# Three weight-chunk splits and the gate-weight splits reordered around the first norm's row factor

## The chip, the cores and the metric

The kernel runs on one core of one Trainium2 chip. Its time is the device time of one execution in microseconds (us), and of several executions the median counts. The engines of the core run side by side, each in the order of its own instruction list, and wait for one another by semaphores: PE is the matrix engine (TensorE), DVE is VectorE, ACT is ScalarE, POOL is GpSimd, and SP issues most of the DMAs.

## The reference

One layer of an encoder on a sequence of 512 tokens of width 1024, all in float32. What matters here is its first part:

```
h    = rms_norm(x, attn_norm_g)
proj = h @ w_in                                  # 1024 -> 2560
xr, gate, q, k, v = split(proj)                  # 512 columns each
xr   = centred_depthwise_conv(xr, conv_w, conv_b)   # 4 taps
h_f  = rg_lru(xr, wa_fwd, ba_fwd, wx_fwd, ...)   # two sigmoid gates, then a scan
h_b  = rg_lru(xr, wa_bwd, ba_bwd, wx_bwd, ...)   # the same, backwards
```

After it come attention, the output projection and the MLP (`relu(h @ w_up)^2 @ w_down`) and a final norm; the change does not touch their code.

## The kernel before

Every float32 product is made of three matmuls. An operand is split into a rounded high part and the remainder (the "rest", or low part), and the helper `mm3` (L222) adds high x high, high x low and low x high in one accumulator. A weight arrives in chunks of 128 x 1024. `emit_dma` (L182) loads a chunk into one of three `wraw` buffers; `conv_hi(i)` (L189) makes the high part `whi` of chunk i on ACT; `conv_lo(i)` (L195) makes its rest `wlo` on DVE and then issues the load of the next chunk into the buffer that it has freed. `whi` and `wlo` have four buffers each.

The list of chunks begins with three that come together with x (0 to 2), then chunk 3 (the last quarter of the columns of xr) and chunks 4 to 7 (the columns of v). Chunks 3, 4 and 5 are loaded first; chunk 6 is loaded when chunk 3 has been split, chunk 7 after chunk 4, chunk 8 after chunk 5.

The order of PE, ACT, DVE and POOL is that of the program text. The stretch around the change goes as follows.

- The first norm is applied late: the products use x times the gain, and the row factor 1/sqrt(mean square + eps) multiplies the results. `rstd_cols` (L305) makes the factor per token as `rcol`: a small DVE instruction `rv`, then a power on POOL (L310). `row_tile` (L313) transposes it on PE (`prow`, L302) and ACT copies it to SBUF as `rrow` (L316). This row is `rstd`.
- `conv_a(t)` (L374) multiplies the t-th quarter of xr, which lies in a PSUM bank, by `rstd` on DVE (`xr`, L376), and ACT makes the first tap `xc` of it (L378). `conv_b(t)` (L381) adds the three other taps with three DVE instructions (L383 to L385). `conv_h(t)` (L387) makes the high part `xch` on ACT, `conv_c(t)` (L391) its rest `xcl` on DVE.
- `gate_weights(t)` (L365) splits the recurrence's gate weights of quarter t: the high part `gwh` on ACT (L368), the rest `gwl` on POOL (L369).
- `next(spc)` (L553) emits thirteen small POOL instructions (`pl`, `sp`, `cneg`, `chalf`, L139 to L145) for two constants of the recurrence.
- `xmm(ks)` (L544) are steps of the fourth quarter of xr on PE.
- Then comes the v loop of 32 steps (L593), each an `mm3`; chunk 4 serves steps 0 to 7, chunk 5 steps 8 to 15. At steps 5, 6, 8, 9, 11, 12, 14 and 15 two gate products `pg` each are woven in (`lru_gate`, L395): sixteen in all, four for each quarter. ACT turns each `pg` into a sigmoid `ga` (L401).

Four PSUM banks (tag "pj") serve the four quarters `pxr` first and then the gate products in turn. So gate product n needs bank n mod 4: the first four wait for the `xr` instructions of quarters 0 to 3, every later one for the sigmoid four products before it. The sigmoids stand in ACT's list in this order: the table load for the sigmoid, two `ga` of quarter 0, `xch` of quarter 2, two more `ga` of quarter 0, `xch` of quarter 3, `conv_hi(6)`, four `ga` of quarter 1, and so on.

Of the kernel before, what the change touches and what calls it, by code (L numbers as in the profile page):

```python
# [72 lines left out]
def hybrid_kernel(ctx: ExitStack, tc, xw, xT, w_in, w_v, w_out, w_up, w_dn, gates, vecs, rel, onehot, fg, out):  # L73
# [13 lines left out]
    def g_(name, dt=FT, shape=(P, S)):  # L87
        return work.tile(list(shape), dt, name=name, tag="g", bufs=NG)
# [4 lines left out]
    def ps_(name, tag):  # L93
        return psum.tile([P, S], FT, name=name, tag=tag, bufs={"pj": 4, "gs": 2, "et": 2}[tag])

    def f(t):
        return t.bitcast(FT)
# [22 lines left out]
    def softplus_consts():  # L120
        ts, tt = nc.gpsimd.tensor_scalar, nc.gpsimd.tensor_tensor
        lam = vt[:, VEC["lam"]:VEC["lam"] + 8]
        e8, sp, z, z2, pl = [small(n, 8) for n in ("e8", "sp8", "z8", "z28", "pl8")]
        cneg = consts.tile([P, 8], FT, name="cneg")
        chalf = consts.tile([P, 8], FT, name="chalf")
        stt(e8, lam, -1.0, lam, op0=OP.mult, op1=OP.max)
        nc.vector.tensor_scalar(sp, lam, -1.0, 0.0, op0=OP.mult, op1=OP.max)
        yield
        act(e8, e8, AF.Exp, scale=-1.0)
        yield  # L130
        nc.vector.tensor_scalar(z, e8, 2.0, None, op0=OP.add)
        nc.vector.reciprocal(z, z)
        tt(z, z, e8, op=OP.mult)
        tt(z2, z, z, op=OP.mult)
        ts(pl, z2, 1.0 / 19, 1.0 / 17, op0=OP.mult, op1=OP.add)
        for c in (15, 13, 11, 9, 7, 5, 3, 1):
            if c == 7:
                yield
            tt(pl, pl, z2, op=OP.mult)  # L139
            ts(pl, pl, 1.0 / c, None, op0=OP.add)  # L140
        tt(pl, pl, z, op=OP.mult)
        ts(pl, pl, 2.0, None, op0=OP.mult)
        tt(sp, pl, sp, op=OP.add)
        ts(cneg, sp, -LRU_C, None, op0=OP.mult)
        ts(chalf, sp, 0.5 * LRU_C, None, op0=OP.mult)  # L145
        yield cneg, chalf

    spc = softplus_consts()
# [28 lines left out]
    def wblock(h, b, q):  # L177
        return w_dn[h, int(b[1]) - 1, (int(b[0]) - 1) * NQ + q]
# [3 lines left out]
    def emit_dma():  # L182
        if plain:
            i = plain.popleft()
            r = stream.tile([P, 1024], FT, name="wraw", tag="wraw", bufs=3)
            nc.sync.dma_start(r, wblock(*chunks[i]) if isinstance(chunks[i], tuple) else chunks[i])
            raws[i] = r

    def conv_hi(i):  # L189
        if i < len(chunks):  # L190
            hi = stream.tile([P, 1024], FR, name="whi", tag="whi", bufs=4)
            act(hi, raws[i], AF.Copy)  # L192
            splits[i] = (hi,)

    def conv_lo(i):  # L195
        if i < len(chunks):
            r = raws.pop(i)
            lo = stream.tile([P, 1024], FR, name="wlo", tag="wlo", bufs=4)
            nc.vector.tensor_tensor(lo, r, f(splits[i][0]), op=OP.subtract)  # L199
            splits[i] += (lo,)  # L200
            c = chunks[i]
            if isinstance(c, tuple) and c[1][0] == "s":
                nxt = {"s1": ("s2", "22"), "s2": ("s4", "21")}.get(c[1])
                if nxt:
                    nc.gpsimd.dma_start(r, wblock(c[0], nxt[1], c[2]), accum_op=OP.add)  # L205
                    raws[C_UP + c[0] * CH + HF + {"s2": 2 * NQ + 2 * c[2], "s4": 6 * NQ + c[2]}[nxt[0]]] = r
            else:
                emit_dma()

    def feed(c, k):  # L210
        if k == 2:
            conv_hi(c + 3)
        elif k == 4:
            conv_lo(c + 3)
# [7 lines left out]
    def mm3(o, a, b, first, last):  # L222
        nc.tensor.matmul(o, lhsT=a[0], rhs=b[0], start=bool(first), stop=False)  # L223
        nc.tensor.matmul(o, lhsT=a[0], rhs=b[1], start=False, stop=False)  # L224
        nc.tensor.matmul(o, lhsT=a[1], rhs=b[0], start=False, stop=bool(last))  # L225
# [119 lines left out]
    def bias_prep():  # L345
        for i in range(2):
            pbz = ps_("pbias", "pj")
            nc.tensor.matmul(pbz[0:NH, :], lhsT=relt, rhs=oht[i], start=True, stop=True)
            nbs = g_("nbs", shape=(NH, S))
            nc.vector.tensor_scalar(nbs, pbz[0:NH, :], -1.0, None, op0=OP.mult)  # L350
            nc.scalar.dma_start(nbd[:, i * S:(i + 1) * S], nbs)
# [3 lines left out]
    def load_tw(h):  # L355
        t = work.tile([P, 1024], FT, name="tw", tag="tw", bufs=4)[:, :896]
        ap = bass.AP(tensor=nbd.tensor, offset=nbd.offset + h * 2 * S, ap=[[1, P], [1, 896]])
        nc.sync.dma_start(t, ap)
        tws[h] = t
# [5 lines left out]
    def gate_weights(t):  # L365
        raw = gwr.pop(t)
        hi, lo = g_("gwh", FR), g_("gwl", FR)
        act(hi, raw, AF.Copy)  # L368
        nc.gpsimd.tensor_tensor(lo, raw, f(hi), op=OP.subtract)  # L369
        gwt[t] = (hi, lo)  # L370
# [3 lines left out]
    def conv_a(t, pp):  # L374
        xr = g_("xr")
        nc.vector.tensor_tensor(xr, pp, rstd, op=OP.mult)  # L376
        c = g_("xc")
        act(c, xr, AF.Identity, scale=vec("w2", t), bias=vec("cb", t))  # L378
        xrt[t], xc[t] = xr, c

    def conv_b(t):  # L381
        xr, c = xrt.pop(t), xc[t]
        stt(c[:, 2:], xr[:, :S - 2], vec("w0", t), c[:, 2:], op0=OP.mult, op1=OP.add)  # L383
        stt(c[:, 1:], xr[:, :S - 1], vec("w1", t), c[:, 1:], op0=OP.mult, op1=OP.add)
        stt(c[:, :S - 1], xr[:, 1:], vec("w3", t), c[:, :S - 1], op0=OP.mult, op1=OP.add)  # L385

    def conv_h(t):  # L387
        xch[t] = g_("xch", FR)
        act(xch[t], xc[t], AF.Copy)

    def conv_c(t):  # L391
        xcl[t] = g_("xcl", FR)
        nc.vector.tensor_tensor(xcl[t], xc[t], f(xch[t]), op=OP.subtract)

    def lru_gate(t, m):  # L395
        hi, lo = gwt[t]
        pg = ps_("pg", "pj")
        sl = slice(m * P, (m + 1) * P)
        mm3(pg, (hi[:, sl], lo[:, sl]), (xch[t], xcl[t]), True, True)
        o = g_("ga")  # L400
        act(o, pg, AF.Sigmoid, bias=vec(("ba0", "bx0", "ba1", "bx1")[m], t))  # L401
        gact[t, m] = o
# [141 lines left out]
    def xmm(ks):  # L544
        for k in ks:
            mm3(pxr[3], wk(3, k), hk(k), k == 0, k == KD - 1)

    conv_hi(3)
    conv_lo(3)
    gate_weights(0)  # L550
    conv_hi(4)
    gate_weights(1)
    cneg, chalf = next(spc)  # L553
    xmm((0,))
    rstd = row_tile(rcol, "et")
    conv_a(0, pxr[0])
    conv_a(1, pxr[1])
    gate_weights(2)
    conv_lo(4)
    xmm((1, 2, 3, 4))  # L560
    conv_b(0)
    conv_h(0)
    conv_a(2, pxr[2])
    gate_weights(3)
    conv_hi(5)
    xmm((5, 6))
    conv_c(0)
    conv_b(1)
# [8 lines left out]
    def lru_hooks(n):  # L577
        m = n - GA
        if m in (11, 12, 14, 15):
            lru_x({11: 0, 12: 1, 14: 2, 15: 3}[m])  # L580
        if m in (12, 13, 20, 22):
            lru_exp({12: 0, 13: 1, 20: 2, 22: 3}[m])
        if m in (16, 17, 27, 28):
            t = {16: 0, 17: 1, 27: 2, 28: 3}[m]
            lru_sqrt(t)
            scans.extend(scan_ops(t)[:4])
        if n in SC:
            scans.popleft()()
# [4 lines left out]
    for n, (k, tt) in enumerate(steps):  # L593
        c = C_V + k // 2
        if k == 0:
            pv[tt] = ps_("pv", vtag[tt])
        hi, lo = splits[c]
        sl = slice((k % 2) * S, (k % 2 + 1) * S)
        tsl = slice(tt * P, (tt + 1) * P)
        mm3(pv[tt], (h_hi[:, k, tsl], h_lo[:, k, tsl]), (hi[:, sl], lo[:, sl]), k == 0, k == KD - 1)  # L600
        if n >= 16:
            feed(c, n % 8)
        if n in (8, 11, 14):
            conv_hi({8: 6, 11: 7, 14: 8}[n])
        if n in (9, 12, 15):
            conv_lo({9: 6, 12: 7, 15: 8}[n])
        if n >= GA and n < GA + 12 and (n - GA) % 3:
            t, m = (n - GA) // 3, 2 * ((n - GA) % 3 - 1)
            lru_gate(t, m)
            lru_gate(t, m + 1)  # L610
        if n == 0:
            conv_lo(5)
            conv_b(2)
        if n == 2:
            conv_b(3)
        if n == GA + 1:
            conv_h(2)
            conv_c(2)
        if n == GA + 2:
            conv_h(3)  # L620
            conv_c(3)
        lru_hooks(n)
        if n == 18:
            bias_prep()
            load_tw(0)
            load_tw(1)
# [665 lines left out]
```

## Time and profile before

| | |
|---|---|
| time, median of 3 runs | 569.79 us (569.21 to 570.31) |
| the profiled execution's own time | 569.28 us |
| its span in the profile | 567.5 us |
| instructions | 6886 |
| granted TensorE clock, mean | 0.996 |
| HBM read, over the span | 78.81 MB, 143 GB/s |

The profile counts microseconds from the start of the span. A row of its timeline gives start and duration in us, engine, line, operation, output and inputs with their shapes, and how many instructions of one kind are merged in the row ("x2"). A bracket at the end tells how long the engine stood idle before the instruction and what ended the wait. A row of a table of stretches gives, for each engine, its busy time in the stretch and its number of instructions.

### The profile page before, as it was taken

What the parts mean: (1) busy time and instruction counts of PE and PEld (TensorE: products, weight loads), DVE (VectorE), ACT (ScalarE), POOL (GpSimd) and SP (SyncE); (2) the same over time, 40 slices, a digit from 0 to 9 for tenths busy, and PEclk for the clock granted to TensorE, in tenths of its full rate; (3) what the DMA queues carried; (4) which work ended last, traced back from release to release, by engine and by line L of the source; (5) the groups of instructions that cost most, each with busy time, mean ns of one, the idle gap of its engine ahead of it and who ended that gap; (6) DMA issues with size and microseconds to landing.
All of it is one profiled execution on the core that took longest, in us unless ns stands there. A gap on an engine that the chain in (4) does not pass through costs nothing.

```text
span 567.5 us, 6886 instructions
## 1 busy us (share of the span) xinstructions
PE 555.4 (98%) x2520; PEld 444.8 (78%) x2520; DVE 388.8 (69%) x610; ACT 313.7 (55%) x510; POOL 50.1 (9%) x70
## 2 busy tenths in 40 slices
PE   9999999999999999999999999999999999999993
PEld 7877788677777768888888888888888888888782
DVE  6696499986865429553468778978243676896894
ACT  7659993687865525245354466653223243665654
POOL 3450000000000000000002133001000000131000
PEclk9999999999999999999999999999999999999998
DMA  7623424453261112242239799959623234699603
GB/s 261 233 74 113 147 102 142 110 160 121 75 223 38 51 59 77 76 148 75 79 111 288 173 268 273 262 174 254 196 74 112 74 112 94 196 252 262 161 1 148
DMA packets 25494, 82.97 MB, mean 146 GB/s; under 512 B 3106, under 2 KB 3234, under 8 KB 25460
## 3 DMA queue, kind: packets, MB, share of 16 engines
q1 hardware_dynamic: 19968, 64.50, 33.1%
q0 software_dynamic: 4608, 16.78, 15.5%
q10 hardware_dynamic: 884, 1.25, 0.6%
q8 instruction: 20, 0.33, 0.2%
q14 instruction: 14, 0.11, 0.1%
HBM read 78.81 MB, written 2.13 MB: 143 GB/s over the span
## 4 chain that ended last, share of the span: by engine, by line
PE 80%; DVE 10%; DMA 4%; ACT 3%; issue 2%; SPq 0%; ACTq 0%; DVEq 0%
PE pu L223 10%; PE pu L224 10%; PE pu L225 10%; PE pd L224 6%; PE pd L223 6%; PE pd L225 6%; PE pqk L223 3%; PE pwo L223 3%; DVE wlo L199 3%; PE pav L751 3%; PE pqk L225 3%; PE pwo L225 3%; PE pwo L224 3%; PE pqk L224 3%; PE pt L718 2%; DMA wraw<-in_w_dn_dram 2%
## 5 line engine op out<-in xcount | busy, mean ns | idle before, releaser
L199 DVE TENSOR_TENSOR wlo<-wraw,whi 128x1024 fp32r<-128x1024 f32 x81 | 99.9, 1234 | 38.4 <-ACT whi L192 38.3
L192 ACT ACTIVATE whi<-wraw 128x1024 fp32r<-128x1024 f32 x81 | 85.5, 1055 | 40.0 <-PE pd L225 17.7
L223 PE MATMUL pu<-h2h,whi 128*128 128x512 f32 x256 | 100.4, 392 | 0.0
L225 PE MATMUL pu<-h2h,wlo 128*128 128x512 f32 x256 | 99.7, 390 | 0.0
L224 PE MATMUL pu<-h2l,whi 128*128 128x512 f32 x256 | 99.6, 389 | 0.0
L224 PE MATMUL pd<-wlo,ah 128*128 128x512 f32 x192 | 74.8, 390 | 0.4 <-DVE wlo L199 0.4
L223 PE MATMUL pd<-whi,ah 128*128 128x512 f32 x192 | 74.7, 389 | 0.0
L225 PE MATMUL pd<-whi,al 128*128 128x512 f32 x192 | 74.7, 389 | 0.0
L1015 ACT ACTIVATE a<-pu 128x512 f32<-128x512 f32 x32 | 19.0, 598 | 97.9 <-PE pu L225 97.9
L1016 DVE TENSOR_TENSOR a<-a 128x512 f32<-128x512 f32 x32 | 22.0, 691 | 65.8 <-ACT a L1015 65.8
L225 PEld LDWEIGHTS pu<-h2h,wlo 128*128 128x128 f32 x256 | 48.0, 188 | 10.1
L223 PEld LDWEIGHTS pu<-h2h,whi 128*128 128x128 f32 x256 | 48.1, 188 | 9.8
L224 PEld LDWEIGHTS pu<-h2l,whi 128*128 128x128 f32 x256 | 48.1, 188 | 9.7
L224 PEld LDWEIGHTS pd<-wlo,ah 128*128 128x128 f32 x192 | 36.0, 188 | 8.1 <-DVE wlo L199 0.8
L223 PEld LDWEIGHTS pd<-whi,ah 128*128 128x128 f32 x192 | 36.0, 188 | 7.5
L225 PEld LDWEIGHTS pd<-whi,al 128*128 128x128 f32 x192 | 36.0, 188 | 7.5
L192 ACT ACTIVATE whi<-ts 128x1024 fp32r<-128x1024 f32 x24 | 25.5, 1060 | 23.7 <-PE pd L225 17.7
L199 DVE TENSOR_TENSOR wlo<-ts,whi 128x1024 fp32r<-128x1024 f32 x24 | 29.3, 1221 | 8.4 <-ACT whi L192 8.0
L223 PE MATMUL pqk<-h_hi,whi 128*128 128x512 f32 x64 | 26.5, 414 | 0.0
L205 POOL DMA_DIRECT2D ts<-in_w_dn_dram x16 | 16.9, 1203 | 106.7 <-DVE wlo L199 106.7
L223 PE MATMUL pwo<-yh,whi 128*128 128x512 f32 x64 | 26.3, 412 | 0.0
L720 ACT ACTIVATE ett<-pt 128x512 f32<-128x512 f32 x32 | 17.3, 591 | 15.7 <-PE pt L718 15.7
(210 smaller groups left out, 1029.5 us busy)
## 6 DMA issues: line engine op xcount, KB each, us to landing
wraw<-in_w_up_dram SPq DMA_DIRECT2D x32, 512.0 KB, 3.3
wraw<-in_w_dn_dram SPq DMA_DIRECT2D x24, 512.0 KB, 6.7
ts<-in_w_dn_dram POOLq DMA_DIRECT2D x24, 512.0 KB, 12.1
wraw<-in_w_in_dram SPq DMA_DIRECT2D x13, 512.0 KB, 3.3
wraw<-in_w_out_dram SPq DMA_DIRECT2D x8, 512.0 KB, 3.3
ts<-in_w_dn_dram SPq DMA_DIRECT2D x8, 512.0 KB, 4.9
tw<-in_w_dn_dram SPq DMA_DIRECT2D x8, 512.0 KB, 6.2
tw<-in_w_dn_dram POOLq DMA_DIRECT2D x8, 512.0 KB, 11.4
```

The lines of the kernel that those rows point to most:

```text
L192: act(hi, raws[i], AF.Copy)
L199: nc.vector.tensor_tensor(lo, r, f(splits[i][0]), op=OP.subtract)
L205: nc.gpsimd.dma_start(r, wblock(c[0], nxt[1], c[2]), accum_op=OP.add)
L223: nc.tensor.matmul(o, lhsT=a[0], rhs=b[0], start=bool(first), stop=False)
L224: nc.tensor.matmul(o, lhsT=a[0], rhs=b[1], start=False, stop=False)
L225: nc.tensor.matmul(o, lhsT=a[1], rhs=b[0], start=False, stop=bool(last))
L718: nc.tensor.transpose(pt[:, qt * P:(qt + 1) * P], en[h][qt][:, jt * P:(jt + 1) * P], ident)
L720: act(t, pt, AF.Copy)
L751: nc.tensor.matmul(pav[p][a, :], lhsT=vs[:, jt, h * DH:(h + 1) * DH], rhs=et.pop((h, jt)), start=jt == 0, stop=jt == 3)
L1015: act(r, p, AF.Relu)
L1016: nc.vector.tensor_tensor(r, r, r, op=OP.mult)
```

## The change

```diff
-    conv_hi(3)
-    conv_lo(3)
+    for i in (3, 4, 5):
+        conv_hi(i)
+    for i in (3, 4, 5):
+        conv_lo(i)
     gate_weights(0)
-    conv_hi(4)
     gate_weights(1)
-    cneg, chalf = next(spc)
     xmm((0,))
     rstd = row_tile(rcol, "et")
     conv_a(0, pxr[0])
     conv_a(1, pxr[1])
     gate_weights(2)
-    conv_lo(4)
+    gate_weights(3)
+    cneg, chalf = next(spc)
     xmm((1, 2, 3, 4))
     conv_b(0)
     conv_h(0)
     conv_a(2, pxr[2])
-    gate_weights(3)
-    conv_hi(5)
     xmm((5, 6))
...
         if n == 0:
-            conv_lo(5)
             conv_b(2)
```

No instruction is added or removed; PE's list is the same. The lists of the other engines change between `rv` and the v loop:

- ACT: before hi3, gwh0, hi4, gwh1, `rrow`, xc0, xc1, gwh2, xch0, xc2, gwh3, hi5, xch1, xc3. After: hi3, hi4, hi5, gwh0, gwh1, `rrow`, xc0, xc1, gwh2, gwh3, xch0, xc2, xch1, xc3.
- DVE: before `rv`, lo3, xr0, xr1, lo4, taps of quarter 0, xr2, xcl0, taps of quarter 1, xr3, xcl1, lo5, taps of quarters 2 and 3. After: `rv`, lo3, lo4, lo5, xr0, xr1, taps of quarter 0, xr2, xcl0, taps of quarter 1, xr3, xcl1, taps of quarters 2 and 3.
- POOL: before `rcol`, gwl0, gwl1, the thirteen small instructions, gwl2, gwl3. After: `rcol`, gwl0, gwl1, gwl2, gwl3, the thirteen small ones.
- SP: its list of DMAs keeps its order; the loads of chunks 7 and 8 become free to go when lo4 and lo5 are done.

Here hi, lo, gwh, gwl, xr, xc, xch and xcl with a number stand for the instruction on chunk or quarter of that number.

## The prediction

> **What bounds the kernel now.** I read the page's busy shares first, then a table of stretches.
>
> ```profile
> PE 555.4 (98%) x2520; PEld 444.8 (78%) x2520; DVE 388.8 (69%) x610; ACT 313.7 (55%) x510; POOL 50.1 (9%) x70
> ...
> 26.00:56.00 30.00, 28.50 (x123) 22.24 (x122) 24.92 (x31) 22.74 (x33) 10.40 (x16) 1.00 0.27 91
> 56.00:101.00 45.00, 45.00 (x195) 36.15 (x194) 34.09 (x42) 34.60 (x46) 0.00 (x0) 1.00 0.40 135
> 210.00:300.00 90.00, 90.00 (x415) 74.42 (x415) 51.17 (x88) 40.40 (x67) 1.01 (x1) 1.00 0.30 103
> ```
>
> PE bounds it. The first number behind each stretch's length is PE's busy time: from 56 us on PE is busy without a gap, but between 26 and 56 us, in the v loop with the gate products, it is 28.50 of 30.00. What PE gains there should reach the end, as everything later is released by PE's results or by buffers freed in the same order. Next, rows picked out of PE's own timeline there, and a row of stretches.
>
> ```profile
> 24.26 0.60 PE L302 MATMUL prow<-ident,rcol 128*128 128x128 f32 x4
> 37.65 0.39 PE L223 MATMUL pv<-whi,h_hi 128*128 128x512 f32 x1
> 38.63 0.50 PE L224 MATMUL pv<-wlo,h_hi 128*128 128x512 f32 x1 [0.60 <-DVE wlo L199]
> 42.16 0.50 PE L223 MATMUL pg<-xch,gwh 128*128 128x512 f32 x1 [0.72 <-ACT ga L401]
> 45.34 0.50 PE L223 MATMUL pg<-xch,gwh 128*128 128x512 f32 x1 [0.18 <-ACT ga L401]
> 45.68 0.40 PE L224 MATMUL pg<-xcl,gwh 128*128 128x512 f32 x1
> ...
> 46.00:55.00 9.00, 9.00 (x41) 7.43 (x40) 4.95 (x7) 8.31 (x13) 0.00 (x0) 1.00 0.51 176
> 55.02 0.39 PE L223 MATMUL pv<-whi,h_hi 128*128 128x512 f32 x1
> ```
>
> Without a wait, 41 matmuls start after 45.68 and up to 55.02, so one starts every 9.34 / 41 = 0.228 us. Between 37.65 and 45.68 lie 25 starts (program order), worth 5.70 us; they took 8.03. So PE loses 2.33 us at three waits: for lo5 at v step 8; for the third `ga` of quarter 0, whose bank the third product of quarter 1 needs; and for the first `ga` of quarter 1. 2.33 us is the most that the change can give at this place.
>
> Why are these late? Rows of DVE's timeline, then of ACT's:
>
> ```profile
> 21.65 1.23 DVE L199 TENSOR_TENSOR wlo<-wraw,whi 128x1024 fp32r<-128x1024 f32 x1
> 25.68 1.29 DVE L376 TENSOR_TENSOR xr<-pxr,rrow 128x512 f32<-128x512 f32 x2 [2.80 <-ACT rrow L316]
> 28.02 0.74 DVE L383 SCALAR_TENSOR_TENSOR xc<-xr,vt,xc 128x510 f32<-128x510 f32 x1
> 33.93 0.68 DVE L376 TENSOR_TENSOR xr<-pxr,rrow 128x512 f32<-128x512 f32 x1
> 34.77 1.57 DVE L393 TENSOR_TENSOR xcl<-xc,xch 128x512 fp32r<-128x512 f32 x1 [0.16 <-ACT xch L389]
> 36.27 2.31 DVE L199 TENSOR_TENSOR wlo<-wraw,whi 128x1024 fp32r<-128x1024 f32 x1
> 38.50 0.74 DVE L383 SCALAR_TENSOR_TENSOR xc<-xr,vt,xc 128x510 f32<-128x510 f32 x1
> 43.80 0.69 DVE L393 TENSOR_TENSOR xcl<-xc,xch 128x512 fp32r<-128x512 f32 x1 [0.16 <-ACT xch L389]
> 34.65 0.82 ACT L378 ACTIVATE xc<-xr,vt 128x512 f32<-128x512 f32 x1
> 35.48 1.28 ACT L401 ACT_TABLE_LOAD   x1
> 36.78 1.27 ACT L401 ACTIVATE ga<-pg,vt 128x512 f32<-128x512 f32 x2
> 40.90 0.63 ACT L389 ACTIVATE xch<-xc 128x512 fp32r<-128x512 f32 x1 [2.86 <-DVE xc L385]
> 41.44 1.25 ACT L401 ACTIVATE ga<-pg,vt 128x512 f32<-128x512 f32 x2
> 44.62 2.41 ACT L401 ACTIVATE ga<-pg,vt 128x512 f32<-128x512 f32 x4
> ```
>
> lo5 (36.27) stands on DVE behind both convolutions, ends at 38.58, and holds up the taps of quarter 2. ACT idles 2.86 us for those taps before xch2, and the two `ga` at 41.44 queue behind it.
>
> **What POOL does to DVE.** The change crowds GpSimd instructions against DVE ones, so their quarrel has to be priced, from rows of POOL's timeline.
>
> ```profile
> 21.82 1.97 POOL L310 TENSOR_TENSOR rcol<-rv,mhalf 128x4 f32<-128x4 f32 x1 [10.32 <-DVE rv L307]
> 23.77 1.29 POOL L369 TENSOR_TENSOR gwl<-gwr,gwh 128x512 fp32r<-128x512 f32 x1
> 25.24 1.30 POOL L369 TENSOR_TENSOR gwl<-gwr,gwh 128x512 fp32r<-128x512 f32 x1 [0.18 <-ACT gwh L368]
> 28.93 0.67 POOL L139 TENSOR_TENSOR pl<-pl,z 128x8 f32<-128x8 f32 x1
> 30.50 0.20 POOL L139 TENSOR_TENSOR pl<-pl,z 128x8 f32<-128x8 f32 x1
> 34.50 3.00 POOL L369 TENSOR_TENSOR gwl<-gwr,gwh 128x512 fp32r<-128x512 f32 x2
> 135.37 1.04 POOL L310 TENSOR_TENSOR rcol<-rv,mhalf 128x4 f32<-128x4 f32 x1 [97.87 <-DVE rv L307]
> ```
>
> gwl2 starts at 34.50; xcl1, asked for at 34.77, takes 1.57 instead of 0.69 (43.80), as if started at 35.65, 0.15 before gwl2's end. gwl3 then waits for xcl1 (3.00 for the pair instead of 2.6), and lo5 for gwl3: 2.31 instead of 1.23. So they take turns: one holds the other up for all but the last 0.15 of its duration, and whoever waits goes next. A tap does the same to a small `pl` (0.67 against 0.20). `xr`, with an input in PSUM, pays nothing: two take 1.29 beside gwl1. And `rcol`, asked for during lo3, takes 1.97 instead of 1.04: it runs when lo3 lets go, at about 22.7.
>
> **The change, part by part.** First the high parts of chunks 4 and 5; the rows are chunk 5's DMA issue, its size and landing time, and ACT's timeline:
>
> ```profile
> 17.15 0.33 SPq L186 DMA_DIRECT2D wraw<-in_w_v_dram  x1
> wraw<-in_w_v_dram SPq DMA_DIRECT2D x1, 512.0 KB, 5.2
> ...
> 19.77 1.06 ACT L192 ACTIVATE whi<-wraw 128x1024 fp32r<-128x1024 f32 x1 [2.19 <-DMA wraw<-in_w_v_dram]
> 23.06 0.63 ACT L368 ACTIVATE gwh<-gwr 128x512 fp32r<-128x512 f32 x1 [2.24 <-DMA gwr<-in_gates_dram]
> ```
>
> - hi4 runs in ACT's idle 2.24 us ahead of gwh0, from 20.72 (chunk 4's landing is what ended ACT's wait at 19.77). hi5 waits for chunk 5: issued 17.15, landed 5.2 later, 22.35; it ends at 23.4. gwh0 moves from 23.06 to 23.36 and gwh1 ends at about 24.5. `rrow` needs `prow`, which ends at 24.86, so it starts at 24.9 and is not late: no cost, hidden by PE's own way to `prow`. Without that cover (chunk 5 later than 22.7 or so) every us of delay is one of `rrow`.
> - Behind lo3, `rcol` is waiting and goes at 22.7, as before, until 23.79; `prow` at 24.26 has 0.4 to spare. lo4, ready at 22.8, is now behind `rcol`. How long a 128x4 power holds DVE up no row shows: DVE was idle after each of the three. Bounds: the smallest `pl` holds next to nothing (0.20 - 0.15 = 0.05), the `gwl` rows all but 0.15 (1.04 - 0.15 = 0.89). I take 0.89: it is the only duration of that size that a row shows DVE waiting out.
> - So lo4 runs 23.6 to 24.8; gwl0 has asked at 24.07 and goes next, to 25.9; lo5 25.8 to 27.05; xr0 at 26.96 instead of 25.68, beside gwl1. The taps of quarter 0 then start at 28.5 instead of 28.02 (lo4 is no longer between). gwl2, after xc1 and gwh2, cuts in between two taps at 29.9, and gwl3 ahead of xcl0. No row shows a tap beside a `gwl`; the bounds are 0 (as `xr`) and 1.15 (as xcl1), and I take 1.15, since a tap's inputs lie in SBUF as xcl1's do and the `pl` wait for it. xr3 comes at 35.6 instead of 33.93 (+1.7), and with it xc3, the table load and the first `ga`: 38.5 instead of 36.78.
> - xcl1 and lo5 no longer pay the 0.88 and 1.08, and lo5 (1.14) is gone from there: the taps of quarter 2 start at 37.1 instead of 38.50 (-1.4). xch2 comes at 39.7 instead of 40.90, the third `ga` at 40.2 instead of 41.44, the first `ga` of quarter 1 at 43.2 instead of 44.62.
> - The thirteen `pl` come behind gwl3 and end at about 41. Their first reader is the recurrence's exponential, on ACT behind all sixteen sigmoids, over 10 us later: nothing. The loads of chunks 7 and 8 start earlier (lo4, lo5), in a queue that has the gate loads already behind it: nothing.
>
> PE in that case: the fourth gate product needs xr3 (36.3, with 0.1 for the semaphore 36.4) at 36.28: 0.13, and 0.11 for the slow restart that each wait row shows (0.34 to the next start instead of 0.228), 0.24. v step 8 finds lo5 ready. The first product of quarter 1, due at 38.56, needs the first `ga` (39.13 + 0.1): 0.67 + 0.11 = 0.78. The third, due at 41.4, finds its bank free at 40.96; the later ones do too. Lost: 1.02 instead of 2.33, a gain of 1.3 us.
>
> **Sum.** 569.28 - 1.3 = 567.98 for the profiled execution, which ran 0.51 below the median of the three; against the median 569.79 - 1.3 = 568.5.
>
> The Trainium skill, "SBUF — State Buffer" ("Who interferes with whom"), has it that a DVE instruction with two SBUF inputs and a GpSimd one that reads SBUF exclude each other for a whole instruction. By that rule `rcol` holds DVE for its full 1.04 us, and the sum would be 569.79 - (1.3 - 0.15) = 568.6; if it lets go early, 567.5. The `gwl` rows agree with the rule, but for the last 0.15 us; no run here shows it for a power.
>
> **The rivals.**
> 1. *`rcol` lets DVE go early* (0.05). Then lo4 starts at 22.8, lo5 at 23.95 just ahead of gwl0's request at 24.07, xr0 at 25.5, xr3 at 34.5, the first `ga` ends at 38.0, before its bank is needed at 38.3, and PE waits nowhere: 569.79 - 2.3 = 567.5. For it: 128x4 is little to read. If gwl0 wins that close race, xr0 comes at 26.2 and about 2.0 is left: 567.8.
> 2. *Starved row factor*: lo3, lo4 and lo5 stand back to back, and `rcol` gets its turn only behind lo5, at 25.1. It ends at 26.2, `prow` stalls 2.1 us, and what the v loop gains is paid there: 569.7, no change. Against it: the `pl` and `gwl3` rows, where the waiting GpSimd instruction went next. A gain given back to a later wait that PE just misses today would look the same.
> 3. *Slower, chunk 5 late*: hi5 now stands ahead of gwh0, gwh1 and `rrow`. Once chunk 5 lands later than 25.1, `rrow`, behind hi5 and two gwh, is 2.3 us late and the gain is gone, and each us more costs one: at 26.5, 1.4 us slower, 571.2. Against it: it landed at 22.35, and nothing ahead of it in its queue has changed.
>
> **Chances.** My forecast (`rcol` holds DVE) 0.45, its own range 568.2 to 568.9; rival 1 0.30; rival 2 0.15; rival 3 or a loss like it 0.10. The range 567.4 to 569.7 takes in rival 1's end and most of rival 2. Within 0.2% (1.14 us) is about what a measurement cannot tell from no change. Rival 1 is faster by more nearly always, my forecast 6 times in 10, rival 2 hardly: 0.57 faster. Rival 2 and the rest of the forecast are the same: 0.33. Slower 0.10.
>
> **What will show it.** `rcol` still ends near 23.8 and `prow` stays at 24.3 (right), or `prow` waits (rival 2). lo4 takes 2.0 us or more (forecast) or 1.23 (rival 1). hi5 starts near 22.4 (or rival 3). The table load comes at 37.2 (forecast) or 36.1 (rival 1). PE's waits for lo5 and for the third `ga` are gone; the forecast leaves one at the first product of quarter 1 of 0.6 to 0.8 us. It is wrong if PE's busy time in the stretch does not rise by about what the span falls, or if a new gap opens behind 56 us.

## The result and the profile after

| | before | after |
|---|---|---|
| median of 6 runs each | 569.62 us (568.42 to 570.35) | 566.26 us (565.79 to 567.36) |
| ratio, 95% interval | | 0.9948 (0.9937 to 0.9958) |
| the profiled execution's own time | 569.28 us | 566.53 us |
| its span | 567.5 us | 564.8 us |

The kernel became faster, clear of the 0.2% bound and by more than was predicted: 568.5 us was forecast and the range ended at 567.4. Two later comparisons of the same two kernels gave 0.9961 (0.9949 to 0.9973) and 0.9963 (0.9951 to 0.9976), so the first one puts the gain high; the sizes below take that into account.

The page's busy shares and the table of stretches of the changed kernel:

```profile
PE 554.5 (98%) x2520; PEld 445.0 (79%) x2520; DVE 388.7 (69%) x610; ACT 313.5 (56%) x510; POOL 51.9 (9%) x70
...
26.00:56.00 30.00, 29.98 (x128) 22.99 (x127) 23.58 (x32) 24.13 (x35) 12.81 (x17) 1.00 0.25 87
56.00:101.00 45.00, 45.00 (x201) 37.02 (x201) 35.05 (x41) 32.80 (x43) 0.00 (x0) 1.00 0.39 135
```

PE is now busy for 29.98 of the 30 us in which it was busy for 28.50. From 56 to 500 us it is busy without a gap in both kernels. Next, PE's timeline of the changed kernel at the only place in the v loop where it still loses anything, and the two ends of the stretch in which the change acts: the transpose of the row factor, and the bias product after v step 18.

```profile
23.80 0.60 PE L302 MATMUL prow<-ident,rcol 128*128 128x128 f32 x4
...
37.42 0.39 PE L224 MATMUL pv<-wlo,h_hi 128*128 128x512 f32 x1
37.64 0.39 PE L225 MATMUL pv<-whi,h_lo 128*128 128x512 f32 x1
38.05 0.51 PE L223 MATMUL pg<-xch,gwh 128*128 128x512 f32 x1
38.40 0.40 PE L224 MATMUL pg<-xcl,gwh 128*128 128x512 f32 x1
...
53.28 1.45 PE L348 MATMUL pbias<-oht,relt 33*8 33x512 f32 x3
```

The first gate product of quarter 1 starts 0.41 us after its predecessor instead of 0.23, and the next 0.35 after it: 0.30 us lost, where before lost 2.33. The stretch from `prow` to `pbias` lasts 53.28 - 23.80 = 29.48 us. In before the transpose starts at 24.26, and the row of its bias product is

```profile
55.79 1.02 PE L348 MATMUL pbias<-oht,relt 33*8 33x512 f32 x2
```

so the stretch lasted 31.53: 2.05 us less. The span fell by 2.7. The other 0.65 lies outside: `prow` itself came 0.46 earlier, and everything behind the bias product took 0.2 less (511.5 us, not 511.7), where a wait for a weight rest in the last product of the MLP, at 533 us, was shorter. Whether these two belong to the change is a question for the experiments.

DVE, then ACT, then POOL of the changed kernel, one fence each, rows picked out:

```profile
21.19 2.36 DVE L199 TENSOR_TENSOR wlo<-wraw,whi 128x1024 fp32r<-128x1024 f32 x2
23.93 1.23 DVE L199 TENSOR_TENSOR wlo<-wraw,whi 128x1024 fp32r<-128x1024 f32 x1 [0.37 <-ACT whi L192]
25.45 1.29 DVE L376 TENSOR_TENSOR xr<-pxr,rrow 128x512 f32<-128x512 f32 x2 [0.30 <-ACT rrow L316]
27.02 1.09 DVE L383 SCALAR_TENSOR_TENSOR xc<-xr,vt,xc 128x510 f32<-128x510 f32 x1 [0.29 <-ACT xc L378]
28.94 1.67 DVE L385 SCALAR_TENSOR_TENSOR xc<-xr,vt,xc 128x511 f32<-128x511 f32 x1
34.46 0.68 DVE L376 TENSOR_TENSOR xr<-pxr,rrow 128x512 f32<-128x512 f32 x1
35.91 0.74 DVE L383 SCALAR_TENSOR_TENSOR xc<-xr,vt,xc 128x510 f32<-128x510 f32 x1
```

```profile
22.83 1.06 ACT L192 ACTIVATE whi<-wraw 128x1024 fp32r<-128x1024 f32 x1 [1.21 <-DMA wraw<-in_w_v_dram]
35.18 0.82 ACT L378 ACTIVATE xc<-xr,vt 128x512 f32<-128x512 f32 x1
36.02 1.28 ACT L401 ACT_TABLE_LOAD   x1
37.31 1.27 ACT L401 ACTIVATE ga<-pg,vt 128x512 f32<-128x512 f32 x2
38.47 0.63 ACT L389 ACTIVATE xch<-xc 128x512 fp32r<-128x512 f32 x1
38.99 1.27 ACT L401 ACTIVATE ga<-pg,vt 128x512 f32<-128x512 f32 x2
```

```profile
21.36 1.97 POOL L310 TENSOR_TENSOR rcol<-rv,mhalf 128x4 f32<-128x4 f32 x1 [9.82 <-DVE rv L307]
24.49 3.08 POOL L369 TENSOR_TENSOR gwl<-gwr,gwh 128x512 fp32r<-128x512 f32 x2 [1.16 <-ACT gwh L368]
28.30 3.46 POOL L369 TENSOR_TENSOR gwl<-gwr,gwh 128x512 fp32r<-128x512 f32 x2 [0.73 <-ACT gwh L368]
```

The reader should look first at 21.19: lo3 and lo4 together take 2.36 us, with no pause between (one rest alone takes 1.23, and rows that follow each other on DVE overlap by up to 0.1), while the power for `rcol` runs until 23.33. The power still waits for lo3 (1.97 instead of 1.04), but does not hold lo4 up. So lo5 starts (23.93) ahead of the first gate split (24.49), which has to wait for it, `xr` starts at 25.45, and the taps of quarter 2 at 35.91 instead of 38.50. The sigmoids no longer stand behind a waiting `xch`: the third one starts at 38.99, not 41.44.

### The profile page after: what moved, and what is told of

Its sections match the earlier page's. It is cut to its first block, busy times and chain, and to the rows that moved or that the text cites. A ratio compares the mean times of both kernels' runs of the same rounds, so it can differ in the third digit from the quotient of the medians.

```text
span 564.8 us, 6888 instructions
## 1 busy us (share of the span) xinstructions
PE 554.5 (98%) x2520; PEld 445.0 (79%) x2520; DVE 388.7 (69%) x610; ACT 313.5 (56%) x510; POOL 51.9 (9%) x70
## 4 chain that ended last, share of the span: by engine, by line
PE 88%; DVE 6%; DMA 2%; ACT 2%; issue 1%; ACTq 0%; DVEq 0%
PE pu L224 10%; PE pu L223 10%; PE pu L225 10%; PE pd L224 6%; PE pd L223 6%; PE pd L225 6%; PE pqk L223 3%; PE pwo L223 3%; PE pav L749 3%; PE pqk L225 3%; PE pwo L225 3%; PE pwo L224 3%; PE pqk L224 3%; PE pt L716 2%; DMA wraw<-in_w_dn_dram 2%; DVE wlo L199 2%
## 5 line engine op out<-in xcount | busy, mean ns | idle before, releaser
L224 PEld LDWEIGHTS pd<-wlo,ah 128*128 128x128 f32 x192 | 36.1, 188 | 7.9 <-DVE wlo L199 0.5
L223 PEld LDWEIGHTS pd<-whi,ah 128*128 128x128 f32 x192 | 36.1, 188 | 7.5
L225 PEld LDWEIGHTS pd<-whi,al 128*128 128x128 f32 x192 | 36.1, 188 | 7.4
```

## The experiments

Theory 1: the gain is what PE no longer loses in the v loop, made by the early chunk rests; and the number of the prediction that put its sum wrong is the time for which the power holds DVE. The rivals: the gate splits' move makes the gain; the walk through DVE and ACT was wrong as a whole; part of the gain lies outside the stretch. The table has the stretch from `prow` to `pbias` in each kernel's profile (start of the one taken from the start of the other) and the timed ratio to before.

| kernel | `prow` | `pbias` | stretch, us | ratio, 95% interval |
|---|---|---|---|---|
| before | 24.26 | 55.79 | 31.53 | |
| before again | 24.58 | 56.44 | 31.86 | 0.9997 (0.9989 to 1.0006) |
| after | 23.80 | 53.28 | 29.48 | 0.9948 (0.9937 to 0.9958) |
| after again | 24.69 | 53.81 | 29.12 | 0.9961 (0.9949 to 0.9973) |
| after, third time | 24.26 | 53.38 | 29.12 | 0.9963 (0.9951 to 0.9976) |
| chunks only | 23.79 | 53.40 | 29.61 | 0.9967 (0.9955 to 0.9979) |
| gates only | 24.43 | 56.43 | 32.00 | 0.9996 (0.9988 to 1.0005) |
| lo5 back | 24.68 | 54.52 | 29.84 | 0.9973 (0.9964 to 0.9982) |
| wait for rcol | 24.42 | 54.86 | 30.44 | 0.9978 (0.9969 to 0.9987) |
| wide power | 25.25 | 54.37 | 29.12 | not timed |
| sigmoid early | 24.24 | 54.77 | 30.53 | 0.9982 (0.9973 to 0.9991) |
| sigmoid first | 23.85 | 53.14 | 29.29 | 0.9963 (0.9949 to 0.9976) |

### Before again, after again, and after a third time

No edit.

> The kernel before, timed against itself. Theory 1 (the whole gain is made in the v loop, and the 0.46 us by which the changed kernel's transpose of the row factor came earlier, 23.80 against 24.26, is chance of the start): ratio 1.000 within 0.001, PE's loss at the three waits again 2.3 us, and the transpose starts anywhere between 23.7 and 24.4. Rival (the changed kernel starts faster by something systematic): the transpose again at 24.26 within 0.1, as in the first profile of before.

> The changed kernel, profiled and timed once more. Theory 1: PE's loss in the v loop again 0.2 to 0.4 us (one wait, at the first gate product of quarter 1), lo3 and lo4 back to back in 2.4 us beside the power for rcol, ratio 0.996 to 0.995 (2.0 us of 569.6 in the v loop is 0.9964). Rival (a systematic faster start or tail adds about 0.7 us): ratio 0.995 or less and the transpose of the row factor again at 23.8.

> The changed kernel a third time. Theory 1 (the change is worth what PE no longer loses between the transpose of the row factor and the bias product: 31.5 and 31.9 us there in two profiles of before, 29.5 and 29.1 in two of after, so 2.4 us, ratio 0.9958; the first comparison's 0.9948 was at the edge of chance): ratio 0.9955 to 0.9965, that stretch 29.1 to 29.5 us. Rival (the first comparison was right and 0.6 us more is gained outside the stretch): ratio 0.995 or less.

PE's work up to `prow` is the same in every kernel of the table, and yet `prow` starts between 23.79 and 25.25 us; PE's waits there are for the first tiles of x and their splits, between 4 and 10 us. The kernel before shows 24.26 and 24.58, the changed one 23.80, 24.69 and 24.26. So the 0.46 us by which it came earlier in the first pair is the chance of the start. (24.58 is outside what either theory expected, as the spread is larger than both took it to be.) Behind the bias product the two profiles of before took 511.7 and 511.4 us to the end of the span, the three of the changed kernel 511.5, 511.3 and 511.5: no gain is made there either, and the wait at 533 us is absent from the second profile of before. The stretch itself is steady: 31.5 and 31.9 against 29.5, 29.1 and 29.1, in the mean 31.7 - 29.2 = 2.5 us, or 0.9956. The two repeats gave 0.9961 and 0.9963, and the interval of the first comparison just reaches that. What the first comparison shows beyond some 2.3 us found no cause in any profile; chance is the likely one, though this is not shown. In the later comparisons the median of before was 569.37 and 568.72 us, not 569.62, and that of the changed kernel 567.05 and 566.70, not 566.26.

PE lost 2.6 us at the three waits in the second profile of before, not 2.3. The changed kernel lost 0.30 us in its first profile and nothing in the two others, where 0.2 to 0.4 was expected again. Rows of the third profile of the changed kernel, PE's, then DVE's (xr3) and ACT's; its `prow` starts where that of the first profile of before does:

```profile
24.26 0.60 PE L302 MATMUL prow<-ident,rcol 128*128 128x128 f32 x4
...
38.10 0.39 PE L225 MATMUL pv<-whi,h_lo 128*128 128x512 f32 x1
38.33 0.39 PE L223 MATMUL pg<-xch,gwh 128*128 128x512 f32 x1
...
34.45 0.68 DVE L376 TENSOR_TENSOR xr<-pxr,rrow 128x512 f32<-128x512 f32 x1
...
36.01 1.28 ACT L401 ACT_TABLE_LOAD   x1
```

The first product of quarter 1 (38.33) starts 0.23 us after its predecessor, which is no wait.

### Chunks only

```diff
     gate_weights(0)
     gate_weights(1)
+    cneg, chalf = next(spc)
     xmm((0,))
...
     gate_weights(2)
-    gate_weights(3)
-    cneg, chalf = next(spc)
...
     conv_a(2, pxr[2])
+    gate_weights(3)
```

(from the changed kernel)

> Only the rests and high parts of chunks 4 and 5 are early; the gate weights' splits and the thirteen small POOL instructions stand as before. Theory 1 (the chunk rests are the cause, the gate splits' move only keeps gwl2 and gwl3 from the taps of quarter 2): lo5's wait at v step 8 is gone, gwl2 and gwl3 start at about 35.4 and 37.1 and each cut in on DVE there, so a wait of 0.5 to 0.6 us is left at the first gate product of quarter 2; gain 1.7 us, ratio 0.9970. Rival (the gates' move makes most of it): gain under 0.8 us.

The stretch was 29.61 us, 2.1 less than before's mean. DVE's timeline of this kernel at the taps of quarter 2, and its POOL row:

```profile
34.30 0.74 DVE L383 SCALAR_TENSOR_TENSOR xc<-xr,vt,xc 128x510 f32<-128x510 f32 x1
35.08 1.66 DVE L384 SCALAR_TENSOR_TENSOR xc<-xr,vt,xc 128x511 f32<-128x511 f32 x1
36.77 1.66 DVE L385 SCALAR_TENSOR_TENSOR xc<-xr,vt,xc 128x511 f32<-128x511 f32 x1
```

```profile
34.55 3.33 POOL L369 TENSOR_TENSOR gwl<-gwr,gwh 128x512 fp32r<-128x512 f32 x2
```

gwl2 and gwl3 cut in on two taps, 0.91 us each (1.66 against 0.75), and PE is left with one wait of 0.43 us at the first product of quarter 2, where theory 1 had 0.5 to 0.6. The chunk rests make most of the gain. What the gates' move adds, some 0.4 us by the stretch, is too small for the timed ratios to tell (0.9967 against 0.9961 and 0.9963).

### Gates only

```diff
     gate_weights(1)
-    cneg, chalf = next(spc)
...
     gate_weights(2)
+    gate_weights(3)
+    cneg, chalf = next(spc)
     conv_lo(4)
...
-    gate_weights(3)
     conv_hi(5)
```

(from the kernel before)

> Only the gate weights' splits move in front of the thirteen small POOL instructions; chunks 4 and 5 stay as before. Theory 1: nothing is gained. gwl2 and gwl3 cut in on the taps of quarter 0 at 28.6 and 30.4, xr3 comes 2 us later than in before, and lo5 no longer pays for gwl3, so the waits are only spread over more products: gain -0.1 us, within 0.4 us of before, ratio 0.999 to 1.001. Rival (the gates' move makes most of the gain): 1 us or more, ratio 0.998 or less.

0.9996, no change. The same two splits now fall on two taps of quarter 0, as DVE's timeline shows:

```profile
29.52 1.66 DVE L384 SCALAR_TENSOR_TENSOR xc<-xr,vt,xc 128x511 f32<-128x511 f32 x1
31.22 1.66 DVE L385 SCALAR_TENSOR_TENSOR xc<-xr,vt,xc 128x511 f32<-128x511 f32 x1
...
36.48 0.68 DVE L376 TENSOR_TENSOR xr<-pxr,rrow 128x512 f32<-128x512 f32 x1
...
37.98 1.22 DVE L199 TENSOR_TENSOR wlo<-wraw,whi 128x1024 fp32r<-128x1024 f32 x1
```

lo5 takes 1.22 now and not 2.31, but starts 1.7 us later. PE loses 2.66 us, in six places instead of three. The rival that gives the gain to the gates' move falls.

### lo5 back

```diff
-    for i in (3, 4, 5):
+    for i in (3, 4):
         conv_lo(i)
...
         if n == 0:
+            conv_lo(5)
             conv_b(2)
```

(from the changed kernel)

> The changed kernel, but chunk 5's rest goes back to its old place, behind the rest of quarter 1's taps. Theory 1: lo5 runs at 35.7 with no GpSimd split beside it (1.23 us, not 2.31) and is there before v step 8; it only delays the taps of quarter 2 by 1.14 us, so the third sigmoid and the sigmoids of quarter 1 come 0.5 to 0.8 us later than in the changed kernel; PE loses 0.6 to 0.7 us, gain 1.6 us, ratio 0.997. Rival (lo5's place is what matters): the wait at v step 8 comes back with 0.3 us or more and the gain is under 1 us.

PE lost 0.63 us in the stretch, in the two places named, and none at v step 8: 0.9973 was measured where 0.997 was expected. With lo4 early and no split beside lo5, it costs its 1.14 us of DVE alone, and PE has room for half of that.

### Wait for rcol

```diff
-    for i in (3, 4, 5):
+    conv_lo(3)
+    held = small("held", 4)
+    nc.vector.tensor_copy(held, rcol)
+    for i in (4, 5):
         conv_lo(i)
```

(from the changed kernel)

> The changed kernel with a 128x4 copy of rcol on DVE between lo3 and lo4, which makes DVE wait for the power's end, as the prediction had assumed. Theory 1 (the prediction's walk was right and only the length of that hold was wrong): lo4 starts at 23.4 to 23.9, gwl0 goes ahead of lo5, xr3 at 35.5 to 35.9, the table load at 37.2 to 37.5, PE loses 1.0 to 1.3 us at the fourth product of quarter 0 and the first of quarter 1; gain 1.0 to 1.3 us, ratio 0.998. Rival (the walk itself is wrong, DVE has room to spare there): gain as in the changed kernel, 2.0 us or more.

This puts the prediction's assumption into the program, with a hold a little longer than it assumed. DVE, ACT and PE rows of this kernel:

```profile
23.98 0.17 DVE L552 COPY held<-rcol 128x4 f32<-128x4 f32 x1 [0.94 <-POOL rcol L310]
24.06 3.47 DVE L199 TENSOR_TENSOR wlo<-wraw,whi 128x1024 fp32r<-128x1024 f32 x2
```

```profile
37.66 1.28 ACT L401 ACT_TABLE_LOAD   x1
38.95 1.27 ACT L401 ACTIVATE ga<-pg,vt 128x512 f32<-128x512 f32 x2
```

```profile
39.69 0.50 PE L223 MATMUL pg<-xch,gwh 128*128 128x512 f32 x1 [0.52 <-ACT ga L401]
```

DVE stands idle for 0.94 us, and lo4 starts 2.24 us after lo3 instead of 1.13 (2.36 - 1.23): 1.1 us later, where the prediction took 0.89. Then the forecast's walk comes true: lo4 and lo5 take 3.47 us with a split between them, the first sigmoid starts at 38.95 (38.5 was forecast), and PE loses 0.32 us at the fourth product of quarter 0 (0.24 forecast) and 0.79 at the first of quarter 1 (0.78). A third loss, 0.15 us for `xcl` at 34.0, was not forecast. The stretch is 30.44 us, 1.3 less than before's mean, which is the gain that was predicted. So the walk was right, and the hold, the one number that was far off in it, made the other 1.2 us (30.44 against 29.2).

### Wide power

```diff
     cneg, chalf = next(spc)
+    half = consts.tile([P, 16], FT, name="half")
+    nc.gpsimd.memset(half, -0.5)
+    wide = consts.tile([P, 16], FT, name="wide")
+    nc.gpsimd.tensor_tensor(wide, ones[:, :16], half, op=OP.pow)
```

(from the changed kernel)

> The changed kernel with a 128x16 power more on POOL behind the thirteen small instructions, at about 41, beside the rests of quarters 2 and 3 and lo6 on DVE; its result is not used. By the 1.03 us of the 128x4 power it should take 1 to 4 us. Theory 1 (a power holds DVE's second input only while it reads, a small part of its time): DVE's instructions beside it keep their 0.69 and 1.23 us within 0.15. Rival (whole duration, as a split holds it): one of them is longer by about the power's duration less 0.15 us, if they overlap.

POOL's row of the wide power, and DVE's rows beside it:

```profile
41.79 3.05 POOL L564 TENSOR_TENSOR wide<-ones,half 128x16 f32<-128x16 f32 x1
```

```profile
41.36 0.68 DVE L393 TENSOR_TENSOR xcl<-xc,xch 128x512 fp32r<-128x512 f32 x1
42.21 0.69 DVE L393 TENSOR_TENSOR xcl<-xc,xch 128x512 fp32r<-128x512 f32 x1 [0.16 <-ACT xch L389]
43.15 1.23 DVE L199 TENSOR_TENSOR wlo<-wraw,whi 128x1024 fp32r<-128x1024 f32 x1 [0.26 <-ACT whi L192]
```

The power runs from 41.79 to 44.84. Two DVE instructions with both inputs in SBUF start inside that time and keep 0.69 and 1.23 us; held for the whole power, the one at 42.21 would have lasted past 45. The rival falls. The 128x4 power itself shows the same in the next kernel, the first of the two with an early sigmoid: there it ran from 21.79 to 22.83, in its 1.04 us, lo3 started beside it at 22.56, and the three rests took 3.50 us, as without a split between them.

### Sigmoid early, and sigmoid first

```diff
+    act(warm, epsb, AF.Sigmoid)
     for i in (3, 4, 5):
         conv_hi(i)
```

(from the changed kernel: the first; the second has the same line ahead of ACT's DMA issues at L338 instead)

> The changed kernel with one more sigmoid, 128x1, ahead of the first high part, so that the table load (1.28 us) falls into ACT's idle time at 17 to 19.6 and not between xc3 and the first sigmoid at 36.0. Theory 1 (the last wait, 0.30 us, is for the first sigmoid, which that load delays): no table load at 36, first sigmoid at about 36.1, no wait at the first product of quarter 1; 0.3 us faster than the changed kernel, gain 2.3 us in the v loop. Rival (the load at 17 pushes the first high part): hi3 starts later than 19.7 and part of it is lost.

> The changed kernel with the extra 128x1 sigmoid ahead of ACT's three DMA issues, where ACT is idle from 17.1 to 19.6, and not behind them as in the first try. Theory 1 (in the first try the table load came behind the DMA issues, at 20.08, pushed the first high part to 21.48, and let the gate splits run into every tap): table load at about 17.5, hi3 at 19.6 to 21.0 as in the changed kernel, first sigmoid at about 36.1 instead of 37.3, no wait at the first product of quarter 1; the stretch from the row factor's transpose to the bias product 29.1 us in this profile; against the changed kernel 0 to 0.3 us faster, ratio to before 0.995 to 0.996. Rival (an early table load costs in itself): slower than the changed kernel by 0.3 us or more again.

The first try lost 1.3 us of the stretch against the changed kernel's 29.2. ACT's timeline shows why:

```profile
19.75 0.29 ACTq L342 DMA_DIRECT2D oht<-in_onehot_dram  x1
20.08 1.28 ACT L548 ACT_TABLE_LOAD   x1 [2.52 <-DMA wraw<-in_w_v_dram]
21.37 0.20 ACT L548 ACTIVATE warm<-epsb 128x1 f32<-128x1 f32 x1
21.48 2.97 ACT L192 ACTIVATE whi<-wraw 128x1024 fp32r<-128x1024 f32 x3
```

ACT's idle time was not free for it. The load reads nothing that a DMA brings, and yet it started only at 20.08, as the DMA issue ahead of it in ACT's list ended (19.75 + 0.29), although the row names the landing of `wraw`. That issue had itself come 2.8 us after the one before it (16.91); what held it up the profile does not show. The high parts came after the load, and the gate splits hit every tap of quarter 0. Put ahead of the DMA issues, the load falls into real idle time. ACT's timeline of the second try:

```profile
17.20 1.28 ACT L338 ACT_TABLE_LOAD   x1
...
35.13 0.82 ACT L379 ACTIVATE xc<-xr,vt 128x512 f32<-128x512 f32 x1
35.85 1.25 ACT L402 ACTIVATE ga<-pg,vt 128x512 f32<-128x512 f32 x2
```

The first sigmoid follows xc3 at once, 1.4 us sooner than in the changed kernel, and the wait at the first product of quarter 1 is gone. The timed ratio is the changed kernel's (0.9963 both, on the same chip), as there was at most 0.30 us to win; its stretch in the one profile is 29.29 us, within the changed kernel's 29.1 to 29.5. No version tried here beats the changed kernel by more than can be measured.

## Why the prediction was wrong

- *What bounds the kernel.* Right. PE's loss of 2.33 us at the three waits was the whole stake at this place; some 2.0 of it came back in the first pair of profiles, all of it in two others, and the later stages passed it on: PE has no gap from 56 to 500 us, and behind the bias product all five profiles took 511.3 to 511.7 us. The sign that the prediction named, that PE's busy time in the stretch should rise by what the span falls, was too strict: busy time rose by 1.48 us where the loss by starts fell by 2.03. Matmuls overlap in the profile (0.39 us each, one started every 0.23), so that a late start counts as idle only beyond the end of its predecessor.
- *The wrong step.* "How long a 128x4 power holds DVE up no row shows ... I take 0.89: it is the only duration of that size that a row shows DVE waiting out." It holds DVE up by nothing that can be seen: lo3 and lo4 stay back to back in 2.36 us. The bounds were 0.05 and 0.89; the choice took for a power what the rows show of a split, which holds DVE up for all but its last 0.15 us. That hold was worth 1.2 us of the sum, as the kernel that waits for `rcol` shows. Why a power leaves DVE free where a split does not was not tried. The rule of the Trainium skill, "SBUF — State Buffer" ("SBUF: two separate sides" and "Who interferes with whom"), that the two exclude each other for a whole instruction, agrees with the trace for the splits, but for their last 0.15 us, and not for the power. This made rival 1 the true case, as written: table load at 36.1 and xr3 at 34.5 were forecast, 36.01 and 34.45 measured in the third profile. The first profile has 36.02 and 34.46, but by luck: there `prow` came 0.46 us early, and `rrow` was 0.4 late behind it.
- *The wait that was left.* In rival 1 PE waits nowhere. So it was in two of the three profiles. In the first one PE had come to `prow` early (23.80), hi5 started no earlier than 22.83, held by chunk 5's landing, and `rrow`, behind hi5 and two gwh on ACT, started 1.04 us after `prow`, against 0.63 and 0.64 in the other two; 0.30 us was left at the first product of quarter 1. That is the case that the prediction named as "without that cover". It is read from the trace; no run was made to force it.
- *Range.* Its low end stood 0.1 us under rival 1's 567.5, and all of it hung on the median of three runs, 569.79. The comparisons later had medians of 568.72 to 569.62 for the same kernel. Rival 1's gain of 2.3 us is 2.4 to 2.5 by the stretch; from 569.62 it ends at 567.2, just outside the range. The other 0.9 us down to the measured 566.26 is not explained by the change's own stretch, and the repeats do not show it.
- *Turns between DVE and POOL.* Right: a waiting split goes next, and a tap pays for it (1.67 against 0.75). The 1.15 assumed for a tap was 0.9. The 0.1 us taken for a semaphore was 0.05: PE started at 38.63 behind lo5's end at 38.58 in before.
- *A reading that was wrong without harm.* The prediction has the landing of chunk 4 end ACT's wait at 19.77. The second `oht` issue stood ahead on ACT and ended at 19.72 (19.42 + 0.30); in the kernel with the early sigmoid a table load that needs no chunk waited for that issue too.
- *Rivals 2 and 3.* `prow` did not wait, and chunk 5 landed early enough in each profile to cost no more than those 0.30 us.

## What to carry to other kernels

Where the sum hangs on one cost with far-apart bounds, let the range reach past both ends, for the nearest row may belong to another kind of instruction. Where two engines hold each other up, price it by a row of the same operation: here a 128x512 split on GpSimd held DVE up for most of its time, and a power of the same engine did not. Moving bulk work off a late chain paid here because the place it went to was idle, as ACT and DVE were before the row factor; moved from one busy stretch of DVE to another, as the gate splits alone, it changed nothing.

## What was not expected of the hardware

- A 128x16 power on GpSimd (3.05 us) ran beside DVE instructions with both inputs in SBUF without lengthening any, while a 128x512 subtraction (1.3 us) lengthened those that waited for all of it by 0.9 to 1.1. At its start the power does wait: 1.97 us behind lo3, 1.04 with DVE idle.
- The same first 23 us of work varied by 1.5 us from one profile to another (`prow` at 23.79 to 25.25), which is most of the gain that was to be measured.
- A DMA issue in ACT's list that came late held all compute behind it on ACT for 2.5 us, though the trace lists that time as idle and names a landing as its end.
